# State-space readout as four products that the matmuls sum, with direction 1 kept in natural order

## The chip, the cores and the metric

One core of a Trainium2 chip runs the whole program. The metric is the device time of one execution in microseconds (us), as the median of the runs; lower is better. The engines are named as the profile names them: PE (TensorE, matrix products), PEld (its weight loads, which overlap PE), DVE (VectorE), ACT (ScalarE), POOL (GpSimd) and SP (SyncE, here the queue that issues the DMAs).

## The reference, cut to what matters

The kernel computes one layer of a diffusion backbone: modulated norm, a state-space branch and an attention branch side by side, a merge, and an MLP. Only the state-space branch is touched:

```python
N_SSM_GROUPS, SSM_STATE, SSM_GROUP = 32, 64, 16
def ssm_discretize(lam_re, lam_im, log_dt, b_re, b_im):
    dt = jnp.exp(log_dt)[:, None]; a_bar = jnp.exp(lam * dt)
    b_bar = ((a_bar - 1) / lam)[..., None] * b
    return a_bar, b_bar
# per direction: states h[n] = a_bar * h[n-1] + b_bar u[n]  (complex, forward or reverse in n)
def ssm_readout(states, c_re, c_im):
    y = jnp.einsum('blgp,ghp->blgh', states, lax.complex(c_re, c_im)).real
y_l = readout(forward states) + readout(backward states) + ssm_d * u_l
```

Each of 32 groups has 16 inputs, 64 complex states and 16 outputs; 1024 latent tokens follow 256 context tokens.

## The kernel before, in words

**Tiling of the branch.** The 1280 tokens are cut into 160 chunks of 8. A pair `q` holds two groups, group `r` of the pair in one half of the partitions (`halves`, 0 to 63 and 64 to 127), so that a tile of 128 partitions is 2 x 64 states. The loop at L864 runs over 16 pairs.

**What one pair does.** `phasors(q)` builds the rotation tables ER and EI of both directions; `pair_params(q)` builds the input weights X and the readout weights CA. In CA the real part goes to partitions 0 to 63 and the imaginary part to 64 to 127, for each `r` (L720 to L727), so that one product with K = 128 sums real and imaginary part. The four 64-partition writes lie on DVE, one on POOL. Four small ACT copies bring the input matrix into the same order (BBs, L732). `pair_xt` transposes X; `pair_u` transposes the inputs of the pair into Ug. `pair_strips(q)` multiplies BBs and CA into the taps of the convolution inside a chunk: four products (L777), then for each `r` one of 16 columns (L781) and one that adds the skip weight (L783), then ACT copies, four DMAs that write strips to DRAM and two that read them back as the matrix M0 (L790, L795). `pair_states(q)` multiplies Ug and XT (L815; direction 1 reads the chunks from the last to the first), rotates the product (four multiplications on DVE, two sums on POOL), runs four scans (L834, L835), rotates back with four multiplications (L840 to L846), and combines the four products into H by eight 64-partition additions (L843, L844, L848, L849), two of them on DVE and six on POOL; direction 1 is turned round while it is written. `pair_out(q)` sums, for each `r`, Ug x M0 (L856) and two products H x CA with K = 128 (L858), and ACT copies the sum into `u_sb` (L859).

**What is interleaved.** The loop is written so that `pair_out` of pair q-1 comes behind `pair_states` of pair q, and two half gates (`gate_half`, 24 matmuls of 512 columns each, L143 to L145) per pair are the dense work between them. Their weights are loaded through SP (L121), split by an ACT copy (L135) and a subtraction on POOL, or on DVE for every fourth (L136). The order on each engine in this stretch isn't written out by hand: a planner orders the instructions by its own estimates of their costs. The queues themselves run strictly in that order.

**Before the loop.** `phasor_powers` (L568 to L587) fills the tables TRe and TIm on DVE, with `tmps[0]` and `tmps[1]` as scratch; `tmps[0]` is used again from L637 on. The discretized input matrices are BbR and BbI (L652).

Of the kernel before, what the change touches and what calls it, by code (L numbers as in the profile page):

```python
# [8 lines left out]
F32 = mybir.dt.float32  # L9
F32R = mybir.dt.float32r  # L10
I32 = mybir.dt.int32
AF = mybir.ActivationFunctionType
OP = mybir.AluOpType
# [9 lines left out]
NG, PS, GH = 32, 64, 16  # L23
# [25 lines left out]
def block_kernel(ctx, tc, io, out, dbg=None):  # L49
    nc = tc.nc  # L50
    V, S, G, T = nc.vector, nc.scalar, nc.gpsimd, nc.tensor
# [109 lines left out]
    psA = psA_.__enter__()  # L161
# [9 lines left out]
    def trb():  # L171
        return psA.tile([128, 512], F32, name="tr", tag="tr", bufs=2)
# [54 lines left out]
    NC_ = 32  # L227

    def pp(name, shape=(128, NC_), dt=F32, p=None):
        return (p or sq).tile(list(shape), dt, name=name)  # L230
# [171 lines left out]
    u_sb = sq.tile([128, NG, 8, GH], F32, name="u_sb")  # L402
# [15 lines left out]
    for q in range(4):  # L418
# [5 lines left out]
        if q == 0:  # L424
# [6 lines left out]
            p = trb()  # L431
            for i in range(3):
# [12 lines left out]
                            op=OP.mult)  # L445
# [22 lines left out]
    tmps = [pp(f"tp{i}", (128, NA, NC_), p=pm) for i in range(4)]  # L468
# [63 lines left out]
    TRe = pp("TRe", (128, NC_, 26))  # L532
# [52 lines left out]
                 *w, t1, t2)  # L585

    phasor_powers()  # L587
    for t in (8, 9):
        load_x(t, st, "xt", 4)

# [21 lines left out]
    for nm in ("re", "im"):  # L612
        p = trb()
# [35 lines left out]
    V.tensor_tensor(t0, nr, lim, op=OP.mult)  # L649
    V.tensor_tensor(fi, fi, t0, op=OP.subtract)  # L650
    V.tensor_tensor(fi, fi, den, op=OP.mult)
    BbR = pp("BbR", (128, NC_, GH))  # L652
    BbI = pp("BbI", (128, NC_, GH))
    bt1, bt2 = [st.tile([128, 512], F32, name="hf", tag="hf", bufs=4).rearrange("p (n h) -> p n h", h=GH)
                for _ in range(2)]
    sh3 = [128, NC_, GH]
# [17 lines left out]
    def col(d, q):  # L674
        return d * 16 + q
# [24 lines left out]
        return tab[:, :, i0:i0 + n, q:q + 1].to_broadcast([128, 2, n, GH])  # L700

    halves = (slice(0, 64), slice(64, 128))
    BBs = [sp1.tile([128, 2, 2, 32], F32, name=f"BB{i}") for i in range(2)]
    for b in BBs:
        G.memset(b, 0.0)

    def pair_params(q):

        X = sp1.tile([128, 2, 2, 8, GH], F32, name="X", tag="X", bufs=1)
        t1 = sp1.tile([128, 2, 8, GH], F32, name="xt1", tag="xt1", bufs=1)  # L710
        t2 = sp1.tile([128, 2, 8, GH], F32, name="xt2", tag="xt2", bufs=1)
        cmul(V, V, X[:, 0], X[:, 1], both(BbR, q, 8), both(BbI, q, 8), pws(PWR, q, 1, 8), pws(PWI, q, 1, 8), t1, t2)

        CA = sp1.tile([128, 2, 2, 10, GH], F32, name="CA", tag="CA", bufs=2)
        cr, ci, pr, pi = both(CT["re"], q, 10), both(CT["im"], q, 10), pws(PWR, q, 0, 10), pws(PWI, q, 0, 10)
        t1 = sp1.tile([128, 2, 10, GH], F32, name="ct1", tag="ct1", bufs=1)
        t2 = sp1.tile([128, 2, 10, GH], F32, name="ct2", tag="ct2", bufs=1)
        G.tensor_tensor(t1, cr, pr, op=OP.mult)
        G.tensor_tensor(t2, ci, pi, op=OP.mult)
        for r, hs in enumerate(halves):  # L720
            V.tensor_tensor(CA[0:64, r], t1[hs], t2[hs], op=OP.add)
        t1 = sp1.tile([128, 2, 10, GH], F32, name="ct1", tag="ct1", bufs=1)
        t2 = sp1.tile([128, 2, 10, GH], F32, name="ct2", tag="ct2", bufs=1)
        V.tensor_tensor(t1, cr, pi, op=OP.mult)
        V.tensor_tensor(t2, ci, pr, op=OP.mult)
        for r, hs in enumerate(halves):
            (G if r else V).tensor_tensor(CA[64:128, r], t2[hs], t1[hs], op=OP.subtract)  # L727

        for c, bb in enumerate((BbR, BbI)):
            bv = bb.rearrange("p (d q) h -> p d q h", d=2)[:, :, q, :]  # L730
            for r, hs in enumerate(halves):
                S.activation(BBs[q % 2][halves[c], r, :, 0:16], bv[hs], AF.Copy)  # L732
        return X, CA

    phasors(0)
# [33 lines left out]

    def pair_strips(q, CA):  # L770
        pS = psA.tile([128, 512], F32, name="s", tag="s", bufs=3)
        BB = BBs[q % 2]

        for d, n in ((0, 128), (1, 112)):
            for r in range(2):
                o = 64 * d + 32 * r
                T.matmul(pS[o:o + 32, 0:n], BB[:, r, d, :], CA[:, r, d, d + 1:9, :], start=True, stop=d == 1,  # L777
                         tile_position=(0, o))
        for r in range(2):
            o = 32 * r  # L780
            T.matmul(pS[o:o + 32, 112:128], BB[:, r, 1, :], CA[:, r, 1, 1, :], start=False, stop=False,  # L781
                     tile_position=(0, o))
            T.matmul(pS[o:o + 32, 112:128], ident[:32, 16 * r:16 * r + 32], deye[:, q, :], start=False, stop=True,  # L783
                     tile_position=(0, o))
        stp = sp.tile([128, 128], F32, name="stp", tag="stp", bufs=1)
        for d, n in ((0, 128), (1, 112)):
            S.activation(stp[halves[d], 0:n], pS[halves[d], 0:n], AF.Copy)
            for r in range(2):
                o = 64 * d + 32 * r
                LD.dma_start(strip_d[q][16 * r:16 * r + 16, 128 * d:128 * d + n], stp[o:o + 16, 0:n])  # L790
        M0 = sp.tile([128, 2, 128], F32, name="M0", tag="M0", bufs=2)
        sd = strip_d[q]
        for r in range(2):
            src = bass.AP(tensor=sd.tensor, offset=sd.offset + r * 16 * 240, ap=[[16, 8], [240, 16], [1, 128]])
            LD.dma_start(M0[:, r, :], src)  # L795
        return M0
# [11 lines left out]
    def pair_states(q, XT, Ug):  # L808
        pr = psA.tile([128, 512], F32, name="s", tag="s", bufs=3)
        pi = psA.tile([128, 512], F32, name="s", tag="s", bufs=3)  # L810
        for d in range(2):
            for c, p in ((0, pr), (1, pi)):
                for r in range(2):
                    mv = Ug[:, r, 0:160] if d == 0 else Ug[:, r, 191:31:-1]
                    T.matmul(p[64 * r:64 * r + 64, d * NCH:(d + 1) * NCH], XT[:, d, c, 64 * r:64 * r + 64], mv,  # L815
                             start=True, stop=True)
        er_, ei_ = Et.pop(q)
        sr = pr[:, :2 * NCH].rearrange("p (d n) -> p d n", d=2)
        si = pi[:, :2 * NCH].rearrange("p (d n) -> p d n", d=2)

        def rt(name, n=NCH, bufs=1):
            return sp.tile([128, 2, n], F32, name=name, tag=name, bufs=bufs)

        t1, t2, t3, t4 = rt("q1"), rt("q2"), rt("q3"), rt("q4")
        V.tensor_tensor(t1, sr, er_, op=OP.mult)
        V.tensor_tensor(t2, si, ei_, op=OP.mult)
        G.tensor_tensor(t1, t1, t2, op=OP.add)
        V.tensor_tensor(t3, si, er_, op=OP.mult)
        V.tensor_tensor(t4, sr, ei_, op=OP.mult)
        G.tensor_tensor(t3, t3, t4, op=OP.subtract)  # L830
        g1, g2 = rt("g1"), rt("g2")
        for d in range(2):
            rr = r8[:, col(d, q):col(d, q) + 1].to_broadcast([128, NCH])
            V.tensor_tensor_scan(g1[:, d, :], rr, t1[:, d, :], 0.0, op0=OP.mult, op1=OP.add)  # L834
            V.tensor_tensor_scan(g2[:, d, :], rr, t3[:, d, :], 0.0, op0=OP.mult, op1=OP.add)  # L835
        H = sp.tile([128, 2, 2, 128], F32, name="H", tag="H", bufs=2)
        w = slice(31, 159)
        t5, t6, t7, t8 = rt("q1"), rt("q2"), rt("q3"), rt("q4")
        m = slice(0, 128)
        V.tensor_tensor(t5[:, :, m], er_[:, :, w], g1[:, :, w], op=OP.mult)  # L840
        V.tensor_tensor(t6[:, :, m], ei_[:, :, w], g2[:, :, w], op=OP.mult)
        for r, hs in enumerate(halves):
            (G if r else V).tensor_tensor(H[0:64, r, 0], t5[hs, 0, m], t6[hs, 0, m], op=OP.subtract)  # L843
            (G if r else V).tensor_tensor(H[0:64, r, 1, ::-1], t5[hs, 1, m], t6[hs, 1, m], op=OP.subtract)  # L844
        V.tensor_tensor(t7[:, :, m], er_[:, :, w], g2[:, :, w], op=OP.mult)
        V.tensor_tensor(t8[:, :, m], ei_[:, :, w], g1[:, :, w], op=OP.mult)  # L846
        for r, hs in enumerate(halves):
            G.tensor_tensor(H[64:128, r, 0], t7[hs, 0, m], t8[hs, 0, m], op=OP.add)  # L848
            G.tensor_tensor(H[64:128, r, 1, ::-1], t7[hs, 1, m], t8[hs, 1, m], op=OP.add)  # L849
        return H  # L850

    def pair_out(q, CA, M0, Ug, H):
        for r in range(2):
            py = trb() if r else psA.tile([128, 512], F32, name="s", tag="s", bufs=3)
            o = py[:, :128]
            T.matmul(o, Ug[:, r, 32:160], M0[:, r, :], start=True, stop=False)  # L856
            for d in range(2):
                T.matmul(o, H[:, r, d, :], CA[:, r, d, 2 * d:2 * d + 8, :], start=False, stop=d == 1)  # L858
            S.activation(u_sb[:, 2 * q + r].rearrange("p s h -> p (s h)"), o, AF.Copy)  # L859

    gate_w = {0: gate_load(0)}
    xts = pair_xt(0, *par)
# [940 lines left out]
```

## Time and profile before

| | us |
|---|---|
| median of 3 runs | 1933.39 (1931.21 to 1934.56) |
| the profiled execution | 1933.46 |
| its span (first to last instruction) | 1931.7 |
| PE busy | 1838.1 (95% of the span) |
| DVE busy | 1315.5 (68%) |
| POOL busy | 989.9 (51%) |
| ACT busy | 705.5 (37%) |

The state-space loop lies between 123 and 407 us. The page's slices of the span show it: DVE stands at 9 tenths in five slices on end there, and mostly at 4 to 7 in the later half of the span.

How to read the rows: "idle before" is the idle time of the engine just before an instruction, with the one that ended it. A matmul of full-precision f32 stands in the trace as two records, so L777 with four matmuls shows x8. Times of consecutive records overlap, since matmuls are pipelined; what one costs in a stream is the distance between starts.

### The profile page before, as it was taken

To read this page: it belongs to the slowest core of one execution; us is meant where nothing else is said; L and a number is where in the kernel's file an instruction comes from. 1 tells how busy PE (TensorE), PEld (TensorE's weight loads), DVE (VectorE), ACT (ScalarE), POOL (GpSimd) and SP (SyncE) were. 2 spreads that over 40 slices of the span, in tenths; PEclk is the share of its full clock that TensorE was granted. 3 is DMA by queue.
4 is the path that set the end of the run, shared out by engine and by line. 5 is a ranking of instruction groups with operands and counts; after the bars stand their busy time and mean duration, and the time that the engine had idled before them with its cause. 6 is when DMAs were issued, how large, how long until landed. Compare 5 with 4: busy or idle time off the path is not lost.

```text
span 1931.7 us, 24218 instructions
## 1 busy us (share of the span) xinstructions
PE 1838.1 (95%) x8674; PEld 1398.4 (72%) x8674; DVE 1315.5 (68%) x2242; ACT 705.5 (37%) x1072; POOL 989.9 (51%) x583
## 2 busy tenths in 40 slices
PE   7889999899989999999998999999999999999998
PEld 4667777778767655565546777887888877878887
DVE  5979999946898777877735447377554556545556
ACT  4452322234313555555552122355434541211110
POOL 2237665622434677777784453276444464443330
PEclk9988999999989999999998999999999999999999
DMA  9321222221222000000004665255554455233213
GB/s 313 87 70 46 65 77 76 68 67 56 83 87 93 17 22 18 23 17 23 23 17 161 215 193 175 97 183 187 157 164 148 133 196 196 94 111 111 88 55 142
DMA packets 179336, 200.65 MB, mean 104 GB/s; under 512 B 28112, under 2 KB 128260, under 8 KB 179216
## 3 DMA queue, kind: packets, MB, share of 16 engines
q1 hardware_dynamic: 179216, 199.11, 32.5%
q8 instruction: 68, 1.11, 0.2%
q14 instruction: 52, 0.43, 0.1%
HBM read 154.85 MB, written 44.09 MB: 103 GB/s over the span
## 4 chain that ended last, share of the span: by engine, by line
PE 47%; issue 9%; POOL 8%; DVE 5%; DMA 2%; ACT 1%; SPq 0%; POOLq 0%; ACTq 0%; DVEq 0%
PE pv L1194 7%; PE mm L143 7%; PE mm L144 7%; PE mm L145 7%; POOL wL L1663 5%; PE sT L1174 4%; PE sT L1177 4%; PE mx L1083 3%; PE mm L1591 1%; PE mm L1592 1%; PE mm L1593 1%; PE mx L1088 1%; DMA wr<-in_w_mod_dram 1%; PE mx L1218 1%; PE mm L210 1%
## 5 line engine op out<-in xcount | busy, mean ns | idle before, releaser
L1199 POOL TENSOR_TENSOR accP<-accP,P 128x1024 f32<-128x1024 f32 x96 | 239.8, 2498 | 21.6 <-ACT P L1181 16.4
L1763 DVE TENSOR_TENSOR acc<-acc,mm 128x512 f32<-128x512 f32 x240 | 162.4, 686 | 127.8 <-PE mm L145 127.8
L136 POOL TENSOR_TENSOR wL<-wr,wH 128x1024 fp32r<-128x1024 f32 (+1 forms) x58 | 135.7, 2348 | 184.7 <-ACT wH L135 180.9
L1181 ACT ACTIVATE P<-sT 128x1024 f32<-128x1024 f32 x160 | 163.8, 1026 | 117.9 <-PE sT L1177 112.4
L1085 DVE TENSOR_REDUCE m<-mx 128x1 f32<-128x512 f32 x240 | 154.5, 686 | 76.1 <-PE mx L1083 69.7
L143 PE MATMUL mm<-wH,sH 128*128 128x512 f32 x480 | 187.8, 391 | 3.2 <-DVE acc L1763 3.2
L145 PE MATMUL mm<-wH,sL 128*128 128x512 f32 x480 | 187.5, 391 | 0.0
L144 PE MATMUL mm<-wL,sH 128*128 128x512 f32 x480 | 187.4, 390 | 0.0
L1194 PE MATMUL pv<-P,Vt 128*64 128x512 f32 x640 | 151.5, 603 | 0.0
L1735 POOL TENSOR_TENSOR sL<-wr,sH 128x1024 fp32r<-128x1024 f32 x30 | 72.2, 2408 | 154.2 <-ACT sH L1734 154.2
L135 ACT ACTIVATE wH<-wr 128x1024 fp32r<-128x1024 f32 (+1 forms) x62 | 62.0, 1005 | 219.9 <-PE mm L144 79.5
L1734 ACT ACTIVATE sH<-wr 128x1024 fp32r<-128x1024 f32 x30 | 31.6, 1054 | 228.4 <-issue 160.7
L143 PEld LDWEIGHTS mm<-wH,sH 128*128 128x128 f32 x480 | 90.5, 189 | 24.1 <-DVE acc L1763 4.4
L1174 PE MATMUL sT<-Q,KH 128*128 128x512 f32 x320 | 105.4, 410 | 2.2 <-ACT P L1181 2.2
L144 PEld LDWEIGHTS mm<-wL,sH 128*128 128x128 f32 x480 | 90.5, 189 | 18.9
L145 PEld LDWEIGHTS mm<-wH,sL 128*128 128x128 f32 x480 | 90.4, 188 | 18.7
L143 PE MATMUL mm<-hH,wH 128*128 128x512 f32 x248 | 102.0, 411 | 0.0
L1177 PE MATMUL sT<-Q,K 65*128 65x512 f32 x320 | 101.3, 397 | 0.0
L145 PE MATMUL mm<-hH,wL 128*128 128x512 f32 x248 | 98.5, 397 | 0.0
L144 PE MATMUL mm<-hL,wH 128*128 128x512 f32 x248 | 98.1, 396 | 0.0
L1663 POOL TENSOR_TENSOR wL<-wr,wH 128x1024 fp32r<-128x1024 f32 x32 | 76.8, 2401 | 36.7 <-ACT wH L1662 36.7
L1194 PEld LDWEIGHTS pv<-P,Vt 128*64 128x64 f32 x640 | 41.9, 137 | 72.7 <-issue 63.4
(582 smaller groups left out, 4799.9 us busy)
## 6 DMA issues: line engine op xcount, KB each, us to landing
wr<-in_w_mlp_dram SPq DMA_DIRECT2D x48, 512.0 KB
wr<-in_w_in_dram SPq DMA_DIRECT2D x35, 512.0 KB
wr<-in_w_mod_dram SPq DMA_DIRECT2D x32, 512.0 KB
s_d<-r SPq DMA_DIRECT2D x64, 256.0 KB
wr<-s_d SPq DMA_DIRECT2D x32, 512.0 KB
rw<-in_w_mlp_dram SPq DMA_DIRECT2D x30, 512.0 KB
x<-in_x_dram SPq DMA_DIRECT2D x12, 512.0 KB
xt<-in_w_mod_dram SPq DMA_DIRECT2D x24, 256.0 KB
```

What stands on the lines that cost most here:

```text
L136: (low or G).tensor_tensor(L[:, :n], raw[:, :n], H[:, :n], op=OP.subtract)
L143: T.matmul(ps, lH, rH, start=i == 0, stop=False)
L144: T.matmul(ps, lH, rL, start=False, stop=False)
L145: T.matmul(ps, lL, rH, start=False, stop=i == n - 1)
L1085: V.tensor_reduce(m3[:, 4 * j + t, c:c + 1], m, axis=AX.X, op=OP.max)
L1174: T.matmul(o, KH[kv][:, ks], Q1[:, j], start=True, stop=False)
L1177: T.matmul(o, K2[kv][:, ks], Q2[:, j], start=False, stop=True)
L1181: S.activation(P, sT, AF.Exp, scale=HD ** -0.5)
L1194: T.matmul(pv[64 * j:64 * j + 64, :], Vt[:, kt, kv * 64:kv * 64 + 64], P[:, j * 512:(j + 1) * 512], start=kt == 0, stop=kt == NK - 1)
L1199: G.tensor_tensor(accP, accP, P, op=OP.add)
L1663: (low or G).tensor_tensor(L[:, :n], raw[:, :n], H[:, :n], op=OP.subtract)
L1763: V.tensor_tensor(a_, a_ if bi else bb2[:, o], ps, op=OP.add)
```

## The change

CA is kept in natural order: one tile of the real part and one of the imaginary part, each with the two groups in their own partition halves, written by one addition and one subtraction of all 128 partitions on DVE. The H tile now holds the four products of the back rotation instead of their two combinations; the eight additions are gone, and the matmuls of `pair_out` sum the products: for each `r` eight with K = 64 instead of two with K = 128, placed in the half of the array's rows that belongs to `r`. The strips are built likewise, with BbR and BbI as they are (with one column block of zeros behind them), eight matmuls for L777 and four for L781, and the BBs tiles and their ACT copies are gone. Direction 1 is no longer turned round: Ug is read forwards, its scans read and write backwards, and its phasor tables are turned round once, by eight ACT copies before the loop.

```diff
     phasor_powers()
+    for tab, tm in ((TRe, tmps[0]), (TIm, tmps[1])):
+        tf = tm.rearrange("p a c -> p (a c)")
+        for a, n in ((0, 16), (16, 10)):
+            t_ = tf[:, 0:16 * n].rearrange("p (c n) -> p c n", n=n)
+            S.activation(t_, tab[:, 16:32, a:a + n], AF.Copy)
+            S.activation(tab[:, 16:32, a:a + n], t_[:, :, ::-1], AF.Copy)
...
-        for r, hs in enumerate(halves):
-            V.tensor_tensor(CA[0:64, r], t1[hs], t2[hs], op=OP.add)
+        V.tensor_tensor(CA[:, 0], t1, t2, op=OP.add)
...
-        for r, hs in enumerate(halves):
-            (G if r else V).tensor_tensor(CA[64:128, r], t2[hs], t1[hs], op=OP.subtract)
-
-        for c, bb in enumerate((BbR, BbI)):
-            bv = bb.rearrange("p (d q) h -> p d q h", d=2)[:, :, q, :]
-            for r, hs in enumerate(halves):
-                S.activation(BBs[q % 2][halves[c], r, :, 0:16], bv[hs], AF.Copy)
+        V.tensor_tensor(CA[:, 1], t2, t1, op=OP.subtract)
...
+        BB = [t.rearrange("p c h -> p (c h)") for t in (BbRz, BbIz)]
         for d, n in ((0, 128), (1, 112)):
-            for r in range(2):
-                o = 64 * d + 32 * r
-                T.matmul(pS[o:o + 32, 0:n], BB[:, r, d, :], CA[:, r, d, d + 1:9, :], start=True, stop=d == 1,
-                         tile_position=(0, o))
+            for c in range(2):
+                for r, hs in enumerate(halves):
+                    o, w = 64 * d + 32 * r, col(d, q) * GH
+                    T.matmul(pS[o:o + 32, 0:n], BB[c][hs, w:w + 32], CA[hs, c, d, d + 1:9, :], start=c == 0,
+                             stop=d == 1 and c == 1, tile_position=(64 * r, o))
+        for c in range(2):
+            for r, hs in enumerate(halves):
+                o, w = 32 * r, col(1, q) * GH
+                T.matmul(pS[o:o + 32, 112:128], BB[c][hs, w:w + 32], CA[hs, c, 1, 1, :], start=False, stop=False,
+                         tile_position=(64 * r, o))
         for r in range(2):
             o = 32 * r
-            T.matmul(pS[o:o + 32, 112:128], BB[:, r, 1, :], CA[:, r, 1, 1, :], start=False, stop=False,
-                     tile_position=(0, o))
             T.matmul(pS[o:o + 32, 112:128], ident[:32, 16 * r:16 * r + 32], deye[:, q, :], start=False, stop=True,
                      tile_position=(0, o))
...
-        H = sp.tile([128, 2, 2, 128], F32, name="H", tag="H", bufs=2)
...
-        for r, hs in enumerate(halves):
-            G.tensor_tensor(H[64:128, r, 0], t7[hs, 0, m], t8[hs, 0, m], op=OP.add)
-            G.tensor_tensor(H[64:128, r, 1, ::-1], t7[hs, 1, m], t8[hs, 1, m], op=OP.add)
+        H = sp.tile([128, 4, 2, 128], F32, name="H", tag="H", bufs=2)
...
+        V.tensor_tensor(H[:, 0], er_, g1, op=OP.mult)
+        V.scalar_tensor_tensor(H[:, 1], ei_, -1.0, g2, op0=OP.mult, op1=OP.mult)
+        V.tensor_tensor(H[:, 2], er_, g2, op=OP.mult)
+        V.tensor_tensor(H[:, 3], ei_, g1, op=OP.mult)
...
+        py = [trb() if r else psA.tile([128, 512], F32, name="s", tag="s", bufs=3) for r in range(2)]
         for r in range(2):
...
-            for d in range(2):
-                T.matmul(o, H[:, r, d, :], CA[:, r, d, 2 * d:2 * d + 8, :], start=False, stop=d == 1)
+            T.matmul(py[r][:, :128], Ug[:, r, 32:160], M0[:, r, :], start=True, stop=False)
+        for d in range(2):
+            for k in range(4):
+                for r, hs in enumerate(halves):
+                    T.matmul(py[r][:, :128], H[hs, k, d, :], CA[hs, k // 2, d, 2 * d:2 * d + 8, :], start=False,
+                             stop=d == 1 and k == 3, tile_position=(64 * r, 0))
```

## Rows read from the trace of the kernel before

**Rows 1.** Busy time by stretch: length, busy us of each engine, PE clock, DMA.

```profile
123.40:184.79 61.39, 54.71 (x326) 44.34 (x326) 53.89 (x115) 16.02 (x40) 43.75 (x37) 0.84 0.19 59
184.79:392.05 207.26, 191.68 (x1178) 157.39 (x1177) 205.51 (x387) 57.97 (x153) 129.34 (x138) 0.98 0.24 71
392.05:407.17 15.12, 11.07 (x66) 9.44 (x65) 5.70 (x14) 2.90 (x7) 11.38 (x14) 0.85 0.28 84
```

**Rows 2.** Waits in 184.79 to 392.05: us in total, times, longest.

```profile
PE s L815 <- DVE Ug L805: 14.7, 9, 2.1
PEld s L815 <- ACT BB L732: 8.7, 4, 2.2
```

**Rows 3.** PE in order of time, fastest pair: start, us, records, idle before.

```profile
184.78 1.31 PE L815 MATMUL s<-Ug,XT 128*64 128x160 f32 x16
186.01 0.49 PE L856 MATMUL s<-M,Ug 128*128 128x128 f32 x2
186.34 0.61 PE L858 MATMUL s<-CA,H 128*128 128x128 f32 x4
186.78 0.39 PE L856 MATMUL tr<-M,Ug 128*128 128x128 f32 x2
...
199.16 0.41 PE L777 MATMUL s<-CA,BB 128*32 128x128 f32 x8
199.40 0.21 PE L781 MATMUL s<-CA,BB 128*32 128x16 f32 x2
199.54 0.23 PE L783 MATMUL s<-deye,ident 32*32 32x16 f32 x2
...
200.03 1.31 PE L815 MATMUL s<-Ug,XT 128*64 128x160 f32 x16
```

**Rows 4.** DVE by line, 184.79 to 392.05: count, busy us, mean ns, idle before.

```profile
L721 DVE TENSOR_TENSOR CA<-ct,ct 64x320 f32<-64x320 f32 x24 | 21.0, 876 | 0.2
...
L727 DVE TENSOR_TENSOR CA<-ct,ct 64x320 f32<-64x320 f32 x12 | 11.8, 985 | 0.4
...
L557 DVE TENSOR_TENSOR ER<-et,et 128x320 f32<-128x320 f32 x11 | 8.2, 747 | 0.0
...
L558 DVE TENSOR_TENSOR et<-TRe,TIm 128x320 f32<-128x320 f32 x11 | 7.0, 632 | 0.4
L843 DVE TENSOR_TENSOR H<-q,q 64x128 f32<-64x128 f32 x12 | 6.5, 538 | 0.0
...
L555 DVE TENSOR_TENSOR et<-TRe 128x320 f32<-128x320 f32 x11 | 5.3, 478 | 0.0
```

**Rows 5.** PE in order of time, the first pairs: idle before, in brackets.

```profile
123.40 0.73 PE L777 MATMUL s<-CA,BB 128*32 128x128 f32 x8 [5.09 <-DVE CA L727]
...
145.25 1.31 PE L815 MATMUL s<-Ug,XT 128*64 128x160 f32 x16 [2.51 <-DVE Ug L805]
...
148.98 1.23 PE L858 MATMUL s<-CA,H 128*128 128x128 f32 x3 [1.76 <-POOL H L848]
```

**Rows 6.** PE in order of time, third pair.

```profile
169.33 0.49 PE L858 MATMUL s<-CA,H 128*128 128x128 f32 x2 [2.41 <-POOL H L849]
```

**Rows 7.** The last pair in order of time: POOL, the DMA queue, then PE.

```profile
393.82 2.38 POOL L136 TENSOR_TENSOR wL<-wr,wH 128x1024 fp32r<-128x1024 f32 x1
...
396.22 0.40 SPq L121 DMA_DIRECT2D wr<-in_w_in_dram  x1
...
402.02 1.62 SPq L795 DMA_DIRECT2D M<-strip_d  x2
...
404.42 0.77 PE L856 MATMUL s<-M,Ug 128*128 128x128 f32 x2 [4.05 <-DMA M<-strip_d]
```

**Rows 8.** Ahead of the loop, in order of time: DVE, ACT, PE.

```profile
92.07 0.19 DVE L639 TENSOR_TENSOR tp<-lam 128x32 f32<-128x32 f32 x1
...
97.56 1.28 ACT L595 ACTIVATE u_sb<-mm 128x512 f32<-128x512 f32 x2 [7.16 <-PE mm L212]
...
100.16 0.44 PE L294 MATMUL tr<-ident,xt 128*128 128x128 f32 x2 [1.43 <-DVE xt L275]
```

More of the change, by code (lines that the diff above doesn't have):

```diff
@@ L651, in block_kernel @@
     V.tensor_tensor(fi, fi, den, op=OP.mult)
-    BbR = pp("BbR", (128, NC_, GH))
-    BbI = pp("BbI", (128, NC_, GH))
+    BbRz = pp("BbR", (128, NC_ + 1, GH))
+    BbIz = pp("BbI", (128, NC_ + 1, GH))
+    for b in (BbRz, BbIz):
+        G.memset(b[:, NC_, :], 0.0)
+    BbR, BbI = BbRz[:, :NC_, :], BbIz[:, :NC_, :]
     bt1, bt2 = [st.tile([128, 512], F32, name="hf", tag="hf", bufs=4).rearrange("p (n h) -> p n h", h=GH)
@@ L702, in block_kernel @@
     halves = (slice(0, 64), slice(64, 128))
-    BBs = [sp1.tile([128, 2, 2, 32], F32, name=f"BB{i}") for i in range(2)]
-    for b in BBs:
-        G.memset(b, 0.0)
     def pair_params(q):
@@ L771, in pair_strips @@
         pS = psA.tile([128, 512], F32, name="s", tag="s", bufs=3)
-        BB = BBs[q % 2]
+        BB = [t.rearrange("p c h -> p (c h)") for t in (BbRz, BbIz)]
         for d, n in ((0, 128), (1, 112)):
-            for r in range(2):
-                o = 64 * d + 32 * r
-                T.matmul(pS[o:o + 32, 0:n], BB[:, r, d, :], CA[:, r, d, d + 1:9, :], start=True, stop=d == 1,
-                         tile_position=(0, o))
+            for c in range(2):
[8 more added lines that the diff above has]
+                         tile_position=(64 * r, o))
         for r in range(2):
             o = 32 * r
-            T.matmul(pS[o:o + 32, 112:128], BB[:, r, 1, :], CA[:, r, 1, 1, :], start=False, stop=False,
-                     tile_position=(0, o))
             T.matmul(pS[o:o + 32, 112:128], ident[:32, 16 * r:16 * r + 32], deye[:, q, :], start=False, stop=True,
@@ L813, in pair_states @@
                 for r in range(2):
-                    mv = Ug[:, r, 0:160] if d == 0 else Ug[:, r, 191:31:-1]
+                    mv = Ug[:, r, 32 * d:32 * d + 160]
                     T.matmul(p[64 * r:64 * r + 64, d * NCH:(d + 1) * NCH], XT[:, d, c, 64 * r:64 * r + 64], mv,
@@ L833, in pair_states @@
             rr = r8[:, col(d, q):col(d, q) + 1].to_broadcast([128, NCH])
-            V.tensor_tensor_scan(g1[:, d, :], rr, t1[:, d, :], 0.0, op0=OP.mult, op1=OP.add)
-            V.tensor_tensor_scan(g2[:, d, :], rr, t3[:, d, :], 0.0, op0=OP.mult, op1=OP.add)
-        H = sp.tile([128, 2, 2, 128], F32, name="H", tag="H", bufs=2)
[L837 to L840, printed above, removed]
@@ L841, in pair_states @@
-        V.tensor_tensor(t6[:, :, m], ei_[:, :, w], g2[:, :, w], op=OP.mult)
-        for r, hs in enumerate(halves):
[L843 to L847, printed above, removed]
-            G.tensor_tensor(H[64:128, r, 0], t7[hs, 0, m], t8[hs, 0, m], op=OP.add)
-            G.tensor_tensor(H[64:128, r, 1, ::-1], t7[hs, 1, m], t8[hs, 1, m], op=OP.add)
+            for g_, t_ in ((g1, t1), (g2, t3)):
+                go, ti = (g_[:, 1, ::-1], t_[:, 1, ::-1]) if d else (g_[:, 0, :], t_[:, 0, :])
+                V.tensor_tensor_scan(go, rr, ti, 0.0, op0=OP.mult, op1=OP.add)
@@ L850, in pair_states @@
+        H = sp.tile([128, 4, 2, 128], F32, name="H", tag="H", bufs=2)
+        er_, ei_, g1, g2 = (t.rearrange("p d n -> p (d n)")[:, 31:291].rearrange("p (d n) -> p d n", d=2)[:, :, 0:128]
+                            for t in (er_, ei_, g1, g2))
+        V.tensor_tensor(H[:, 0], er_, g1, op=OP.mult)
+        V.scalar_tensor_tensor(H[:, 1], ei_, -1.0, g2, op0=OP.mult, op1=OP.mult)
+        V.tensor_tensor(H[:, 2], er_, g2, op=OP.mult)
+        V.tensor_tensor(H[:, 3], ei_, g1, op=OP.mult)
         return H
@@ L852, in pair_out @@
     def pair_out(q, CA, M0, Ug, H):
+        py = [trb() if r else psA.tile([128, 512], F32, name="s", tag="s", bufs=3) for r in range(2)]
         for r in range(2):
-            py = trb() if r else psA.tile([128, 512], F32, name="s", tag="s", bufs=3)
-            o = py[:, :128]
-            T.matmul(o, Ug[:, r, 32:160], M0[:, r, :], start=True, stop=False)
-            for d in range(2):
-                T.matmul(o, H[:, r, d, :], CA[:, r, d, 2 * d:2 * d + 8, :], start=False, stop=d == 1)
-            S.activation(u_sb[:, 2 * q + r].rearrange("p s h -> p (s h)"), o, AF.Copy)
+            T.matmul(py[r][:, :128], Ug[:, r, 32:160], M0[:, r, :], start=True, stop=False)
@@ L861, in block_kernel @@
+        for d in range(2):
[3 more added lines that the diff above has]
+                             stop=d == 1 and k == 3, tile_position=(64 * r, 0))
+        for r in range(2):
+            S.activation(u_sb[:, 2 * q + r].rearrange("p s h -> p (s h)"), py[r][:, :128], AF.Copy)
     gate_w = {0: gate_load(0)}
```

## The prediction

> **What bounds the kernel now.** I read the page's busy shares first: PE is busy 95% of the span, so at first sight nothing that relieves DVE or POOL can help. The slices show where that average hides something: only in the state-space loop does DVE reach 9 tenths. So the next view is busy time by stretch. From the states of the fourth pair to those of the last, 184.79 to 392.05 us, lie twelve pairs, and DVE is busy 205.51 of 207.26 us; PE is busy 191.68 [rows 1]. A pair takes 207.26 / 12 = 17.27 us and DVE is its clock. The waits agree: PE waits 14.7 us for Ug, whose last piece is a small DVE copy (L805) stuck in the DVE queue, and 8.7 us of its weight loads are put down to the BBs copies [rows 2]. PE is close behind: the fastest pair took 15.25 us, from 184.78 to 200.03 [rows 3]. That is the number to beat: **PE has about 2 us of slack in each pair, and the change gives DVE time back and asks PE for more.** Behind the loop PE is busy without pause (the chain that ended last runs through PE and POOL there), so what the loop gains or loses reaches the end nearly whole.
>
> **The sum** is made against the profiled execution, 1933.46 us (span 1931.7); it differs from the median, 1933.39, by nothing that matters.
>
> **What DVE loses.** For CA, two 64-partition additions of 876 ns and a subtraction of 985 ns become one addition and one subtraction of 128 partitions; the same form elsewhere takes 478 ns (L555) [rows 4]. Per pair 2 x 0.88 + 0.99 - 2 x 0.48 = 1.8 us. The additions into H go: L843 alone is 0.54 us [rows 4]. And the rotation products that stand beside POOL's additions run at 632 to 747 ns where the same form takes 478 ns (L557 and L558 are two of four such lines) [rows 4]; without those additions each should fall back, some 0.2 x 4 = 0.8 us. Together 3.1 us or more: DVE falls from 17.1 to about 14 us per pair. It has to fall below PE's new need to matter no more, and it does by a good margin. The products, the scans and their count stay; reversed scans and a `scalar_tensor_tensor` in place of a plain product show no reason in these rows to cost more, and 0.1 us each would be covered.
>
> **What PE gains in work.** Price of a record: four full-width records of 128 columns took 186.34 to 186.78, so 0.11 us each [rows 3]. Column tiles run side by side: the eight records of L777 need 0.24 us (199.16 to 199.40) where eight in a row would need 0.88, and sixteen of 160 columns need 1.23 us (184.78 to 186.01), about two at a time [rows 3]. No row of before shows two **row** halves side by side, and that is the unknown on which the forecast hangs.
>
> `pair_out`: 8 records of L858 per pair become 32, half as deep. If the halves r = 0 and r = 1 run side by side, that is 16 x 0.11 = 1.76 for 0.88: +0.88. If they don't, 32 x 0.11 = 3.52: +2.64. Below +0.88 it can't be, since each half alone needs its sixteen streams. I take the low end: the nearest rows are the column tiles, which do overlap. Two changes of tile shape are new (full to half and back to the gates). L856 right behind L815 took 0.33 us for two records (186.01 to 186.34) where 0.22 is the price, so a change costs 0.1: +0.2 [rows 3]. Bounds 0 and 0.3. So +1.06.
>
> `pair_strips`: L777 goes from 8 to 16 records on the same four places of the array. They come as direction 0, then direction 1; seven rounds of 0.11 instead of 0.24, +0.53. The bound below is +0.2 (all four places filled in each round), above +1.5 (16 in a row). In return the two column products and the two skip products no longer alternate: the four groups took 199.40 to 200.03, 0.16 each, mostly change of shape, and three groups' worth remain: -0.16 [rows 3]. So +0.4, and PE's need becomes 15.25 + 1.06 + 0.4 = **16.7 us a pair**. I add 0.15 for waits that a planner's order always leaves.
>
> A sentence of the Trainium skill speaks against the strips: "TensorEngine Tiling (Array Packing)", section "Restrictions and Gotchas", says that different row tiles can't access the same PSUM bank at a time, and here both halves write one tile `pS`. By it the strips would cost the +1.5 end; this is a rival below. In `pair_out` the two halves write two banks. No run here shows the rule yet.
>
> **The steady stretch.** 12 x (16.85 - 17.27) = **-5 us**. PE now sets the pace, DVE and POOL have 3 us to spare.
>
> **The first pairs**, 123.40 to 184.79, are worse than the rest: the mean granted clock is 0.84 [rows 1]; PE waits 2.51 us for Ug, 1.76 us for H from POOL [rows 5] and 2.41 us for H again [rows 6]. The two waits for POOL go (-4.2), H now comes straight from DVE; of the first I count 1.5, as DVE's queue ahead of that copy is shorter by the additions into CA and H. Behind each such wait the clock stood at half, 1.2 GHz; 16% of 61 us is 10 us of lost clock, and I count 2 us of it back. The start waits 5.09 us for the last CA subtraction on DVE [rows 5]; with one addition and a quicker subtraction ahead it ends 0.7 us earlier. PE's added work: two readouts and four strips, 2 x 1.06 + 4 x 0.4 = +3.7. Together **-4.7 us**; bounds -10 and +4.
>
> **Ahead of the loop** eight ACT copies are new. ACT is idle for 7.16 us up to 97.56 [rows 8], which hides them. But `tmps[0]` is then read by ACT, and DVE's first instruction that writes it again (L639, at 92.07) must wait for the first four copies. Queued behind it on DVE are the norm of the context tiles, and PE already waits for those (1.43 us at 100.16) [rows 8]. So what DVE waits, PE waits: **+1 us**, between 0 and 2.5.
>
> **The last pair.** PE idles 4.05 us until M0 lands at 404.42. The strips' DMAs stand on SP behind a weight load (396.22) that waits until POOL has done its subtraction (393.82 + 2.38), which stood behind POOL's additions into H [rows 7]. Those gone, the subtraction, the load and with them the strips' write and read (402.02) move forward by up to 4 us. The half gate ends at about 400, so PE's idle time nearly vanishes; the longer readout takes 1.1 back: **-3 us**, between -4 and +1. The four ACT copies into BBs per pair, the zero block and the two `py` tiles taken at once count as nothing: ACT is busy 57.97 of 207.26 us [rows 1], so its relief frees no engine that sets the pace; the wait put down to BBs [rows 2] is in the slack already.
>
> Sum: -5 - 4.7 + 1 - 3 = -11.7, so 1921.8; I say **1922 us**.
>
> **The rivals.**
>
> *Row halves one behind the other in `pair_out`* (slower). The weights of a half are still 128 columns wide; if loads or streams of the two halves take turns, each record costs 0.11. PE's need is 15.25 + 2.64 + 0.2 + 0.4 = 18.5, the pair 18.65: 12 x 1.38 = +16.6 in place of -5; 1.76 more for each readout in the first pairs and the last: -1.2 and -1.2; +1. Sum +15: **1949**. It decides from about 80 ns a record on: the gain of 11.7 is used up when 15 readouts cost 0.78 us more each, which is 0.024 on each of 32 records at 0.055. For it: no row shows row halves overlapped. Against it: column tiles overlap in every such row.
>
> *Strips one behind the other* (the bank rule). +1.5 - 0.16 = 1.34 instead of 0.4, 0.94 x 16 = +15 on the forecast: **1937**, by the edge of what can be told.
>
> *A new wait takes DVE's place.* M0 comes back through SP behind loads that wait for POOL [rows 7], and the planner orders everything anew; if the strips' read sets the pace, the steady stretch stays at 17.27 and only the first pairs give: -4.7 + 1 + 0 = -3.7, **1930**. Against it: POOL has less to do, so the loads come earlier.
>
> **How the numbers follow.** Forecast 0.6 (its own range 1908 to 1930), halves in turn 0.17, strips in turn 0.1, new wait 0.13. A measurement tells 0.2% (3.9 us, 1929.5 and 1937.3) from no change. Faster: 0.57 of the forecast and half of the new wait, 0.63. Same: 0.03, half of the strips and the other half of the new wait, 0.15. Slower: 0.17 + 0.05 = 0.22. The range goes from 1908 (first pairs at their full -10, the steady stretch at 16.2 a pair) to 1950, a little beyond the slow rival's point.
>
> **What would show it.** Right: in the stretch of twelve pairs DVE well under 90% busy, the pair at 16.5 to 17, no wait of PE for Ug; the two records of r = 0 and r = 1 in L858's successor start within some ns of each other, and 32 of them take about 1.8 us; the first pairs without waits for H; M0 in the last pair before the half gate ends. Wrong: 32 records in 3 us or more, L777 in more than 1 us, PE idle for M0 in each pair, or a DVE idle gap over 2 us near 92 us.

## The result and the profile after

The changed kernel takes **1909.44 us** (median of 4 runs, 1906.34 to 1913.12) where the kernel before takes 1933.97 (4 runs): ratio 0.9877, 95% interval 0.9856 to 0.9897. The forecast was 1922, 11.7 us less than before; it became 24.5 us less, inside the range but twice the gain. The profiled execution took 1909.88 us, its span is 1908.2, so the two profiles lie 23.6 us apart.

The first view is again busy time by stretch (start and end in us, length, then busy us of PE, PEld, DVE, ACT, POOL, the granted PE clock, the DMA share and GB/s). The first stretch begins at 123.40 as in [rows 1] (here the strips of the first pair begin at 123.00); the others are cut at the states (L819) of the fourth and of the last pair.

```profile
123.40:178.70 55.30, 54.17 (x430) 43.70 (x428) 52.99 (x110) 13.44 (x29) 20.94 (x17) 0.94 0.24 73
178.70:376.80 198.10, 198.10 (x1612) 164.62 (x1608) 171.78 (x352) 46.56 (x108) 66.63 (x57) 1.00 0.25 77
376.80:390.00 13.20, 13.20 (x121) 11.31 (x118) 5.29 (x12) 3.60 (x9) 4.05 (x3) 1.00 0.16 54
```

The engines have changed places. In the twelve pairs PE is busy 198.10 of 198.10 us at a clock of 1.00, and DVE, which was busy 205.51 of 207.26 in [rows 1], now has 26 us to spare. A pair takes 198.10 / 12 = 16.51 us instead of 17.27. POOL's busy time fell from 129 to 67 us. The longest waits of that stretch (us in total, times, longest) no longer hold any of PE:

```profile
POOL ct L725 <- DVE CA L732: 65.8, 11, 6.0
...
DVE q L829 <- PE s L819: 13.9, 10, 2.7
...
PEld s L778 <- DVE xt L559: 2.1, 6, 0.4
```

Now DVE waits for PE's states (13.9 us), where PE waited 14.7 us for DVE's Ug in [rows 2]. The only waits on PE's side are loads of weights held for 0.4 us at most.

DVE by line in the same stretch (count, busy us, mean ns, idle before):

```profile
L557 DVE TENSOR_TENSOR X<-xt,xt 128x256 f32<-128x256 f32 x12 | 25.2, 2098 | 0.1
...
L732 DVE TENSOR_TENSOR CA<-ct,ct 128x320 f32<-128x320 f32 x12 | 5.8, 480 | 0.0
...
L557 DVE TENSOR_TENSOR ER<-et,et 128x320 f32<-128x320 f32 x11 | 5.3, 479 | 0.0
...
L847 DVE SCALAR_TENSOR_TENSOR H<-EI,g 128x256 f32<-128x256 f32 x12 | 5.0, 413 | 0.0
```

The subtraction into CA costs 480 ns on 128 partitions where one of 64 cost 985 [rows 4]; L557 is back at 479 from 747 [rows 4]; the product with the sign costs no more than a plain one (L848 takes 414). Of the four 64-partition writes into CA of before, three lay on DVE and one on POOL (L721, L727).

PE in order of time, a steady pair (start, us, engine, line, records):

```profile
178.72 1.31 PE L819 MATMUL s<-Ug,XT 128*64 128x160 f32 x16
179.96 0.49 PE L855 MATMUL s<-M,Ug 128*128 128x128 f32 x2
180.28 0.39 PE L855 MATMUL tr<-M,Ug 128*128 128x128 f32 x2
180.60 0.37 PE L859 MATMUL s<-CA,H 64*128 64x128 f32 x1
180.60 0.37 PE L859 MATMUL tr<-CA,H 64*128 64x128 f32 x1
180.81 0.27 PE L859 MATMUL s<-CA,H 64*128 64x128 f32 x1
180.82 0.27 PE L859 MATMUL tr<-CA,H 64*128 64x128 f32 x1
...
182.38 0.27 PE L859 MATMUL s<-CA,H 64*128 64x128 f32 x1
182.38 0.27 PE L859 MATMUL tr<-CA,H 64*128 64x128 f32 x1
182.58 0.50 PE L143 MATMUL mm<-hH,wH 128*128 128x512 f32 x1
...
194.39 0.41 PE L778 MATMUL s<-CA,BbR 64*32 64x128 f32 x8
194.63 0.39 PE L778 MATMUL s<-CA,BbI 64*32 64x128 f32 x8
194.85 0.21 PE L783 MATMUL s<-CA,BbR 64*32 64x16 f32 x4
194.91 0.22 PE L783 MATMUL s<-CA,BbI 64*32 64x16 f32 x4
195.06 0.24 PE L787 MATMUL s<-deye,ident 32*32 32x16 f32 x4
195.23 1.04 PE L819 MATMUL s<-Ug,XT 128*64 128x160 f32 x12
```

Two things are to be seen. In the readout, the records of r = 0 (into `s`) and r = 1 (into `tr`) start within 7 ns of each other, and sixteen such couples go from 180.60 to 182.58. In the strips, all products with BbR come first and all with BbI after, though the code has the direction as its outer loop: the order in which they stand on PE is not that of the source.

Where the 23.6 us between the two profiles lie: the states of the first pair start 1.8 us later (135.1 for 133.3; 0.9 of it stands already at 25 us, ahead of the new ACT copies); from there to the states of the fourth pair −7.8 (43.7 for 51.5); the twelve pairs −9.2; from the last states to the start of the last record of the last readout −3.3 (11.8 for 15.0). That record thus begins 18.5 us earlier (388.6 for 407.1). The attention branch behind it starts 20.3 us earlier (591.1 for 611.5), and the stretch from there to the end is 3.3 shorter (1317.0 for 1320.3).

### The profile page after: what moved, and what is told of

The parts are those of the page before. It is cut to its first block, busy times and chain, and to the rows that moved or that the text cites. A ratio compares the mean times of both kernels' runs of the same rounds, so it can differ in the third digit from the quotient of the medians.

```text
span 1908.2 us, 25109 instructions
## 1 busy us (share of the span) xinstructions
PE 1841.1 (96%) x9250; PEld 1402.6 (74%) x9250; DVE 1279.1 (67%) x2194; ACT 691.9 (36%) x1016; POOL 895.4 (47%) x471
## 5 line engine op out<-in xcount | busy, mean ns | idle before, releaser
L136 POOL TENSOR_TENSOR wL<-wr,wH 128x1024 fp32r<-128x1024 f32 (+1 forms) x58 | 135.9, 2351 | 197.9 <-ACT wH L135 187.0
```

The source lines that it names most:

```text
L136: (low or G).tensor_tensor(L[:, :n], raw[:, :n], H[:, :n], op=OP.subtract)
```

## The experiments

Unless said otherwise each is the changed kernel with one edit. "Last readout" is the start of the last record of `pair_out`, 407.1 before and 388.6 in the changed kernel.

**Row halves one behind the other.** Is it the overlap of the two row halves that makes twice the records affordable? The same records, but all of r = 0 ahead of all of r = 1:

```diff
-        for d in range(2):
-            for k in range(4):
-                for r, hs in enumerate(halves):
+        for r, hs in enumerate(halves):
+            for d in range(2):
+                for k in range(4):
```

> The changed kernel, with the sixteen products of the readout ordered group by group: all eight of r = 0, then all eight of r = 1, so that the two row halves of the array can't run side by side; nothing else differs. Theory (the halves share the time only when they alternate, and PE sets the pace): 32 records at 0.11 us instead of 16 pairs, +1.76 us for each of 16 pairs, of which the last two or three may be hidden: 26 to 28 us above the changed kernel's 1909, about 1936, with the pair at 18.3 us. Rival (the halves overlap whatever the order, or PE isn't the bound): within 4 us of the changed kernel.

Measured: 1935.11 us, ratio to before 1.0006 (0.9996 to 1.0015): the whole gain is gone by an order of loops. The pair takes 17.95 us, 1.44 more. One readout of it, PE in order of time:

```profile
305.30 0.49 PE L855 MATMUL s<-M,Ug 128*128 128x128 f32 x2
305.62 0.39 PE L855 MATMUL tr<-M,Ug 128*128 128x128 f32 x2
305.94 1.71 PE L859 MATMUL s<-CA,H 64*128 64x128 f32 x13
307.39 0.37 PE L859 MATMUL tr<-CA,H 64*128 64x128 f32 x1
...
307.82 1.61 PE L859 MATMUL tr<-CA,H 64*128 64x128 f32 x13
309.37 0.50 PE L143 MATMUL mm<-hH,wH 128*128 128x512 f32 x1
```

Thirteen records of r = 0 go alone for 1.45 us, a few of both overlap where the two halves meet, thirteen of r = 1 go alone. So 305.30 to 309.37 is 4.07 us for 2.62. The price of 0.11 for a record that goes alone is confirmed, and with it the mechanism of the prediction's first rival, though not its size (1949, a pair of 18.65); the changed kernel escapes it since its halves alternate. Up to the last readout the order of loops costs 19.9 us (408.5 for 388.6). Another 7.1 lie between the first attention product and the end of this profile (1324.2 us for 1317.0), a stretch that the edit doesn't touch (see the scratch, below), and so aren't shown to come from it.

**Does DVE still matter, and how much slack has it?** Three, and seven, idle additions of 128x512 on DVE behind the products into H:

```diff
+        hf = H.rearrange("p k d n -> p (k d n)")
+        jk = sp.tile([128, 512], F32, name="jk", tag="jk", bufs=1)
+        for _ in range(3):
+            V.tensor_tensor(jk, hf[:, 0:512], hf[:, 512:1024], op=OP.add)
         return H
```

> The changed kernel with three idle additions of 128x512 on DVE in each pair, right behind the products of H, about 0.6 us each, 1.8 us a pair. In the changed kernel DVE is busy 171.8 of 198.1 us in twelve pairs, 2.2 us free in each. Theory (PE sets the pace, DVE has 2 us to spare): at most 4 us above the changed kernel, the pair still 16.5 us. Rival (DVE is still what the loop waits for): +1.8 us for each of 16 pairs, 29 us, about 1938.

> As the run with three idle additions, but with seven: 4.2 us of DVE in each pair. Theory: DVE needs 14.3 + 4.2 = 18.5 us a pair and becomes the clock again: the pair at about 18.5 us, some 30 us above the changed kernel, about 1939; and PE shows waits for DVE in each pair again. Rival (DVE work in this loop is hidden whatever it is): within 4 us of the changed kernel. Rival (all of it is exposed): 16 x 4.2 = 67 us, about 1976.

Measured: 1917.47 us with three (last readout 393.8) and 1943.2 with seven (ratio to before 1.0048, 1.0033 to 1.0064; last readout 414.6). With three, the pairs take 16.5 to 17.2 (the last of the twelve 17.9), and DVE is busy 198.82 of 204.60 us:

```profile
177.40:382.00 204.60, 200.38 (x1610) 163.81 (x1608) 198.82 (x393) 46.60 (x108) 82.77 (x59) 1.00 0.26 76
```

An addition takes 680 ns, so three are 2.0 us per pair, and the slack is 26.3 / 12 = 2.2. It is as good as used up, and PE begins to wait (4.2 us in eight pairs for CA). So 8.0 us are lost where the theory allowed 4, but far less is lost than the 3 x 0.68 x 12 = 24 us that an engine setting the pace would have cost. With seven, the twelve pairs take 18.35 us in the mean, close to the expected 18.5, but not for the expected reason. DVE is busy only 191.29 of 220.20 us, 15.9 a pair:

```profile
182.60:402.80 220.20, 206.94 (x1613) 168.61 (x1611) 191.29 (x442) 46.60 (x108) 144.04 (x57) 0.97 0.24 71
```

The waits (us in total, times, longest) and POOL by line show what fills the rest:

```profile
DVE g L840 <- POOL q L831: 28.8, 12, 3.0
...
PE s L778 <- DVE CA L732: 13.3, 10, 2.0
```

```profile
L725 POOL TENSOR_TENSOR ct<-cre,PWR 128x320 f32<-128x320 f32 x11 | 84.3, 7664 | 69.8 <-DVE CA L732 69.8
```

A POOL product of 882 ns in the changed kernel lasts 7664 ns here, and what stands behind it on POOL (L831) makes DVE's scans wait. So the time follows the load on DVE, but by way of POOL; that the number came out near 18.5 is luck. More on this in the last section.

**Which half of the change pays?** The natural order lets two additions of all 128 partitions on DVE do what eight of 64 did. Then PE has 16 readout records per pair, as deep as before in sum, instead of 32:

```diff
-        H = sp.tile([128, 4, 2, 128], F32, name="H", tag="H", bufs=2)
+        H = sp.tile([128, 2, 2, 128], F32, name="H", tag="H", bufs=2)
...
+        V.tensor_tensor(H[:, 0], t5, t6, op=OP.subtract)
+        V.tensor_tensor(H[:, 1], t7, t8, op=OP.add)
...
-            for k in range(4):
+            for k in range(2):
```

(t5 to t8 hold the four products.)

> The changed kernel, but the four products of the back rotation are combined before the readout, by two additions of all 128 partitions on DVE in natural order, and the matmuls sum two products for each r and direction instead of four: 8 pairs of records instead of 16. Theory (PE sets the pace; natural order is what relieved DVE and POOL, not the sums on PE): PE gets 0.88 us a pair back, DVE takes 0.7 to 0.8 more and has 2.2: the pair at 15.6 to 15.8 us, 12 to 14 us below the changed kernel, about 1896. Rival (the loop needs the additions away from DVE): DVE's 15.1 us and its waits set the pace again, no gain or a loss of up to 10 us, 1909 to 1919.

Measured: 1901.35 us, ratio to before 0.9828 (0.9813 to 0.9843), 8.1 us faster than the changed kernel. The pair takes 15.61 us for most of the loop, as expected: 16.51 less eight couples of 0.112. The time misses the expected 1896 by 5 us all the same. The last readout starts at 375.5, 13.1 us earlier; 5 us of that are not seen in the time. In its profile 3.6 of them stand between the first attention product and the end (1320.6 us for 1317.0), a stretch that the change doesn't touch and that varies by as much (see the scratch, below). So of the two halves of the change it is the natural order that pays, together with what hangs on it (the strips without BBs, direction 1 not turned round), which no run takes apart. Letting the matmuls sum costs 0.9 us per pair on the engine that now sets the pace, for work that DVE has room for.

The other side of the same question, the sums as before (eight additions of 64 partitions, two on DVE and six on POOL), but in natural order and with the same 16 records:

```diff
+        for r, hs in enumerate(halves):
+            for d in range(2):
+                (G if r else V).tensor_tensor(H[hs, 0, d], t5[hs, d], t6[hs, d], op=OP.subtract)
+        for r, hs in enumerate(halves):
+            for d in range(2):
+                G.tensor_tensor(H[hs, 1, d], t7[hs, d], t8[hs, d], op=OP.add)
```

> The changed kernel with H combined as in the kernel before, by eight 64-partition additions, two on DVE and six on POOL, but into natural order, and two products for each r and direction in the readout. So CA, the strips and direction 1 are as in the change, and only the sums are as before. It tells which half of the change relieved DVE. Theory (both halves did, CA's 1.8 us a pair more than the sums' 1.3 or more): DVE falls from 17.1 to about 15.5 us a pair with the additions' disturbance, just under PE's 15.6 to 15.7; the pair at 15.7 to 16.5, a time of 1900 to 1912. Rival (the additions on POOL were the trouble by themselves, through the DVE instructions that they hold up and through late H): the pair at 16.8 or more, waits of PE for H in the first pairs, 1918 to 1928.

Measured: 1920.03 us, ratio 0.9936 (0.9915 to 0.9957), some 19 us slower than with two sums on DVE although PE has the same records. That is in the rival's range; the theory's 1912 is passed. The fourth to the eighth pair take PE's 15.61 us, the third takes 23.6, and from the ninth on nearly each takes 17.0 to 17.1, with PE waiting for H (waits, then PE in order of time, then POOL by line; waits and lines from 260 us on):

```profile
PE tr L866 <- POOL H L856: 4.6, 6, 0.8
```

```profile
166.62 0.49 PE L866 MATMUL tr<-CA,H 64*128 64x128 f32 x2 [3.05 <-POOL H L853]
...
282.10 0.45 PE L866 MATMUL s<-CA,H 64*128 64x128 f32 x2
283.33 0.37 PE L866 MATMUL tr<-CA,H 64*128 64x128 f32 x1 [0.78 <-POOL H L856]
```

```profile
L856 POOL TENSOR_TENSOR H<-q,q 64x128 f32<-64x128 f32 x34 | 19.2, 582 | 1.1
L725 POOL TENSOR_TENSOR ct<-cre,PWR 128x320 f32<-128x320 f32 x7 | 17.2, 2460 | 25.2 <-DVE CA L732 25.2
```

The six POOL additions stand in a queue behind L725, which takes 2460 ns here. Ahead of the readout in the third pair it takes 9.93 us:

```profile
155.40 9.93 POOL L725 TENSOR_TENSOR ct<-cre,PWR 128x320 f32<-128x320 f32 x1 [3.56 <-DVE CA L732]
```

The additions into H come only behind it, and PE waits 3.05 us for them at 166.62. That pair alone makes 8 of the 19 us. So the old form of the sums was a cost of its own, beside the order of the partitions.

**The scratch of the eight ACT copies.** Ahead of the loop the copies use `tmps`, and DVE's next write to them waits:

```profile
95.06 0.19 DVE L646 TENSOR_TENSOR tp<-lam 128x32 f32<-128x32 f32 x1 [2.11 <-ACT TRe L594]
```

With tiles of their own:

```diff
-    for tab, tm in ((TRe, tmps[0]), (TIm, tmps[1])):
-        tf = tm.rearrange("p a c -> p (a c)")
+    rvs = [pp(f"rv{i}", (128, 256), p=pm) for i in range(2)]
+    for tab, tf in ((TRe, rvs[0]), (TIm, rvs[1])):
```

> The changed kernel with two scratch tiles of their own for the eight ACT copies that turn the phasor tables, in place of the scratch that DVE writes next. In the changed kernel DVE waits 2.11 us for ACT there, and the first states come 1.8 us later than before. Theory (that wait reaches the end through the norm of the context tiles): 1.5 to 2.5 us below the changed kernel, about 1907.5. Rival (something else is late next, such as ACT, whose copies stand ahead of the context tiles' squares): no difference above 0.5 us, 1909.

Measured: 1909.79 us (ratio 0.9881, 0.9863 to 0.9899), no different from the changed kernel. The wait is gone, the first states start at 131.7 instead of 135.1 (1.3 of these 3.4 us stand already ahead of the place of the wait) and the last readout at 384.6 instead of 388.6. But from the first attention product to the end this profile takes 1320.4 us, the changed kernel's 1317.0. That stretch was between 1317.0 and 1324.2 us in the ten profiles of this case, with the same work in each, so one profile can't tell whether 3 us gained ahead of it are lost in it each time. Part of that spread is TensorE's clock: the time lost to the lower of its two levels (1.2 instead of 2.4 GHz), added up from the granted clock in this stretch, is 9.8 us in the changed kernel, 11.3 here and 14.9 in `rows_apart`, which has the longest stretch. Whether the scratch is worth anything stays open.

**Both together, and one sum given back to POOL.** Two sums and own scratch tiles; the second kernel has the second sum on POOL:

```diff
-        V.tensor_tensor(H[:, 1], t7, t8, op=OP.add)
+        G.tensor_tensor(H[:, 1], t7, t8, op=OP.add)
```

> The two additions on DVE in natural order (pair at 15.6 us, 1901) together with the own scratch tiles: the candidate for a faster kernel. Theory: the gains add up, 1899 to 1900. Rival (as for the scratch alone): 1901.

> As the run with two additions and own scratch, with the second addition on POOL instead of DVE. Theory (PE sets the pace at 15.6 us and DVE has some slack left): the same within 2 us; the last pairs, where the run with both on DVE showed 16.2 us, may gain 1 us. Rival (a POOL addition holds up DVE's two-input instructions beside it by its own length): DVE is no freer than with both, and H comes later: 1 to 3 us more.

Measured: 1898.38 us (1897.07 to 1899.92; ratio 0.9823, 0.9803 to 0.9843) and 1907.33 (ratio 0.9872). The first is the fastest kernel of the case, 11 us ahead of the changed one; its stretch of twelve pairs:

```profile
176.80:364.30 187.50, 187.50 (x1420) 153.77 (x1416) 182.47 (x377) 46.51 (x108) 81.88 (x56) 1.00 0.27 81
```

PE and DVE are nearly level now, PE at 187.50 of 187.50 us and DVE at 182.47. It is 3.0 us below the two sums alone, but that the scratch did this isn't shown: the last readouts start 0.6 us apart (374.9 and 375.5), and 2.2 us lie between the first attention product and the end.

With the second sum on POOL the time is 9 us longer, where the theory said 2 at most and the rival 1 to 3. DVE is no freer for it, as the rival had it, busy 182.16 us of the same length:

```profile
176.80:364.30 187.50, 187.17 (x1414) 153.56 (x1414) 182.16 (x365) 46.52 (x108) 87.12 (x67) 1.00 0.26 79
```

The steady pair is 15.61 in both. The last readout starts 5.3 us later (380.1), and this is lost at the two ends of the loop: the third pair takes 17.30 us, and from the last states to the last readout it is 14.2 us for 10.5. There PE waits for H and for M (PE in order of time):

```profile
164.19 0.37 PE L862 MATMUL s<-CA,H 64*128 64x128 f32 x1 [1.39 <-POOL H L852]
...
376.81 0.66 PE L858 MATMUL s<-M,Ug 128*128 128x128 f32 x2 [2.17 <-DMA M<-strip_d]
```

## Why the prediction came out as it did

**What bounds the loop: right.** PE took DVE's place, DVE fell to 171.78 / 12 = 14.3 us per pair (14 was said), and the gain per pair is DVE's old pace less PE's new need. That PE sets the pace now is shown from both sides: the pair grows by 1.44 us when PE's records go one behind the other (`rows_apart`) and shrinks by 0.90 when PE has eight couples less (`sum_on_dve`). `dve_plus7` shows the reverse only in part: with DVE loaded again the pair is back above its old 17.27, at 18.35, but by way of POOL. One reading was too strong: DVE reaches 9 tenths in the slices not only in the loop but also in the one from 48 to 97 us, which changes nothing in what follows.

**`pair_out`: right in kind, 0.2 low.** It went from 1.36 us (186.01 to 187.37 in the profile of before) to 2.62 (179.96 to 182.58): +1.26 for the forecast's +1.06 (0.88 + 0.2 is in fact 1.08). The couples cost the 0.112 us foreseen; the changes of shape cost 0.3, the upper bound, which is half of what is missing, since three places show one and not two: 180.28 to 180.60 is 0.32 for two records, the first couple takes 0.21, and 182.38 to 182.58 is 0.20. The unknown on which the forecast hung is settled by `rows_apart`.

**`pair_strips`: the step that failed.** I had +0.4; measured is −0.03 (194.39 to 195.23 is 0.84, in [rows 3] 199.16 to 200.03 is 0.87). "Seven rounds of 0.11" took the order of the source for the order on PE. The sixteen records stand as eight of BbR and eight of BbI, each eight fill all four places in two rounds, and together they take 0.46 us for 0.24 before: the +0.2 that I had named as the lower bound. The three groups with small products fell from 0.63 to 0.38 us, −0.25 where I had −0.16. What follows for the pair: 16.85 − 0.43 − 0.15 (the waits I had added; there are none) + 0.2 = 16.47, measured 16.51. Over twelve pairs that is −4.1, and the steady stretch came to −9.2 instead of −5.

The Trainium skill's "TensorEngine Tiling (Array Packing)", section "Restrictions and Gotchas", forbids different row tiles the same PSUM bank at a time. The trace doesn't agree: the strips of both r go into one tile `pS`, in different partitions, and sixteen records need 0.46 us. One behind the other they would need 16 x 0.11 = 1.76, and with the two row halves in turns, but the two column places of a half beside each other, 8 x 0.11 = 0.88. The rival of 1937 that I had built on it falls. It was priced too high as well: the sentence bars row tiles and not column tiles, so I would estimate 0.88 for it, which is 0.08 a pair above the forecast.

**The first pairs: right in kind, too careful.** −7.8 for −4.7. The waits of PE (idle before, in brackets) that are left up to 178.7:

```profile
123.00 0.41 PE L778 MATMUL s<-CA,BbR 64*32 64x128 f32 x4 [3.39 <-DVE CA L727]
...
145.72 1.31 PE L819 MATMUL s<-Ug,XT 128*64 128x160 f32 x16 [1.03 <-DVE Ug L809]
```

The two waits for H in [rows 5, 6] are gone, the one for Ug shrank from 2.51 to 1.03. The second and third pair already take 16.50 and 16.51 us, at a granted clock of 1.00. Before, they were these stretches (columns as in the first fence above):

```profile
145.25:164.98 19.73, 17.97 (x99) 14.70 (x99) 17.19 (x40) 3.46 (x7) 15.05 (x14) 0.83 0.07 21
164.98:184.79 19.81, 17.40 (x102) 14.09 (x100) 19.02 (x41) 4.75 (x13) 15.90 (x14) 0.91 0.18 58
```

There the clock (the length of a stretch times what its granted clock lacks to 1.00) was worth 19.73 x 0.17 + 19.81 x 0.09 = 5.1 us, and all of it came back; I had counted 2 us in all of the first pairs. This is the term of the sum that was mis-sized, by about 3 us.

**Ahead of the loop: right.** +1 was said, between 0 and 2.5. DVE waits 2.11 us at the place named, for seven of the eight copies and not four, as both tables' copies stand in turn; 0.8 to 1.8 us arrive at the first states. An idle time of DVE over 2 us near 92 us was one of the prediction's signs of being wrong; it came true here, and the term still holds within its bounds. That removing the wait shows nothing in the time (`own_scratch`) leaves this term without a proof at the end of the span.

**The last pair: right.** −3 was said, −3.3 measured. The read of M is issued at 379.74 where it stood at 402.02 in [rows 7], PE's idle 4.05 us are gone, and POOL's subtraction now comes after the read (queue of SP, then POOL):

```profile
379.74 1.61 SPq L799 DMA_DIRECT2D M<-strip_d  x2
```

```profile
387.44 2.36 POOL L136 TENSOR_TENSOR wL<-wr,wH 128x1024 fp32r<-128x1024 f32 x1 [6.82 <-ACT wH L135]
```

In the twelve pairs before it PE waits for M nowhere, so the rival of a new wait in DVE's place falls too.

**Behind the loop: not forecast.** 5.1 us more were gained there in these two profiles. Some 1.0 of them has a cause in the rows: before, PE's first gate products behind the last readout ran at the lower clock level after the idle 4.05 us (granted 0.50, 1.2 GHz, from 402.59 to 409.42; 407.17 to 409.44 for five starts, 2.27 us where the changed kernel needs 1.26 from 388.80 on), and now no idle time precedes them. The 3.3 us behind 591 us lie within what that stretch varies by from profile to profile. So of the 11.9 us that the profiles gained beyond the forecast, 7 lie up to the last readout, in the strips, the waits and the clock of the first pairs, and 5 behind it, mostly unexplained. Those 5 us are luck, as far as the prediction goes.

## What to carry to other kernels

Here, where an engine with 99% busy time in a stretch was relieved, the new pace was the need of the next one, read from the fastest pass that the trace holds; work added to that next engine was paid in full, so put it where there is slack (here two additions on DVE instead of sixteen more records on PE). Small products on halves of the array were cheap only where halves that may overlap stood next to each other in the queue: the same records cost 1.44 us per pair more with the loops the other way round. And small additions of 64 partitions on POOL cost more than their sum: DVE's work beside them is stretched [rows 4], and so are they (in `eight_sums` four take 1.78 us at 167.05 and 2.48 at 179.02, beside more of DVE's work).

## What the runs showed of the hardware

**A POOL product can be starved by DVE.** In `dve_plus7`, POOL and then DVE in order of time:

```profile
236.03 8.65 POOL L725 TENSOR_TENSOR ct<-cre,PWR 128x320 f32<-128x320 f32 x1 [6.38 <-DVE CA L732]
```

```profile
236.40 0.48 DVE L558 TENSOR_TENSOR et<-TRe,TIm 128x320 f32<-128x320 f32 x1
236.80 0.69 DVE L853 TENSOR_TENSOR jk<-H 128x512 f32<-128x512 f32 x1
...
242.83 1.22 DVE L136 TENSOR_TENSOR wL<-wr,wH 128x1024 fp32r<-128x1024 f32 x1
243.96 0.49 DVE L829 TENSOR_TENSOR q<-s,ER 128x320 f32<-128x320 f32 x1
```

L725 began at 236.03 and ended at 244.68, all through a run of DVE instructions of two inputs each that followed one another without a gap, at their free durations of 0.42 to 0.69 us (1.22 for the large L136). It came through only as L829 began, the first of that run that has one of its inputs (`s`) in PSUM. From the sixth of its sixteen runs on L725 lasts 5.7 to 8.7 us in each. In the 9.93 us of `eight_sums` DVE had no gap either, until 164.70, 0.63 us before L725's end. In the changed kernel the same product takes 882 ns, and there the other side pays: DVE's L557 takes 2098 ns in the mean for some 420, since in most pairs it stands beside POOL's L136 and lasts as long, 2.6 us. The Trainium skill's "SBUF — State Buffer", section "Who interferes with whom", says that a DVE instruction with two inputs in SBUF contends with a POOL instruction that reads SBUF, that the ports they share are an exclusive lock, and that the order of issue decides who blocks. The trace agrees on who collides with whom; but here the blocked one waited through the whole run, not for one instruction.

**Row halves of one PSUM bank.** Products of the two row halves that write different partitions of one tile in one PSUM bank (`pS`) ran side by side, four places at a time: sixteen records in 0.46 us. No run shows two row halves writing the same partitions of one bank side by side.
